# Attention probabilities normalised head by head in a hybrid decoder layer

## The chip, the cores and the metric

The kernel runs on one core of one Trainium2 chip. A core has a tensor engine (PE), a vector engine (DVE), a scalar engine (ACT), a general engine (POOL) and a queue that mostly issues DMAs (SP); each works through its own instructions in program order and waits for the others by semaphores. The metric is the time of the program on the device in microseconds (us). Three runs before the change took 1918.72, 1920.54 and 1920.89 us; the median is 1920.54 us.

## What is computed

One decoder layer on 2048 tokens with 1024 channels: a combined input projection, three mixers side by side (sliding-window attention, short convolution, trailing means), an output projection and a squared-ReLU MLP, with RMS norms around them. The change lies in the attention:

```python
scores = jnp.where(valid[None, :, None, None], scores + bias, NEG)
m = jnp.maximum(jnp.max(scores, axis=-1, keepdims=True), sink)
p = jnp.exp(scores - m)
denom = jnp.sum(p, axis=-1, keepdims=True) + jnp.exp(sink - m)
probs = (p / denom).astype(v.dtype)
out = jnp.einsum('bnhgqk,bnkhd->bnqhgd', probs, v_band)
```

There are 8 query heads and 2 key/value heads. A query block of 128 tokens sees its own 128 keys and the 128 before. The sink adds one column to the denominator.

## The kernel before

Everything is float32. A product of matrices is made of three matmuls on operands that are split into a rounded part and a remainder (`mm3`, L273 to L276: hi by hi, hi by lo, lo by hi). The rounded part of a weight tile is written by ACT (L252, tile `wh`), the remainder (L253, tile `wl`) mostly by POOL, at some places by DVE.

The tokens run in four blocks of 512 (b = 0 to 3). A block has 14 tiles of the input projection (`pj`, eight k-steps of three matmuls each), then 8 tiles of the output projection (`po`). Between the projection tiles lies the attention, in units of one query tile of 128 tokens (j = 0 to 3) and one KV head (g = 0, 1) with its four query heads: a head group. A block has 8 of them, the program 32. The code staggers them: the scores of one unit, the transposes of the unit two tiles back, and its product with the values stand around one projection tile.

A unit runs through the engines like this. PE writes the scores of four heads into PSUM (L582, L583, tile `sc`). For each head DVE adds the bias, scales, and takes the row's extreme (L592, tiles `s` and `nm`); ACT writes the exponential in place and its row sum (L596, tile `den`, which includes the sink's column 256 of `s`, put there by POOL in L585). Then DVE inverts the sums (L599, `rd`) and multiplies the probabilities (L600). PE transposes them per half of the keys (L610, tile `pt`, two PSUM buffers), ACT rounds (L613, `pth`), DVE takes the remainder (L614, `ptl`), PE multiplies by the values (L621, L622, `av`), and ACT and DVE put the result together (L629 to L635, tiles `ao`, `mxh`, `mxl`), which the output projection reads.

DVE does much else between these: in block 0 it scales each projection tile (L523, `z`), in all blocks it works on convolution (L652, `cy`; L659) and means (L694, L700, L701, tile `po`), and on the norm (L318 to L327: small instructions of 128x4). In block 3 it prepares the MLP's operands as well (L769, L815).

The order of the instructions on each engine isn't that of the code: a scheduler places them when the program is built. So a change of a few instructions can reorder others.

Of the kernel before, what the change touches and what calls it, by code (L numbers as in the profile page):

```python
# [15 lines left out]
ALU = mybir.AluOpType  # L16
# [4 lines left out]
P = 128  # L21
# [63 lines left out]
def tile_trunk(  # L85
# [14 lines left out]
    pe, act, dve, gp, sp = nc.tensor, nc.scalar, nc.vector, nc.gpsimd, nc.sync  # L100
# [75 lines left out]
    for j, (r, what) in enumerate(plan):  # L176
# [4 lines left out]
        else:  # L181
            n = what[1]
# [391 lines left out]
    def att_scores(b, j, g):  # L574
        k0 = P if (b == 0 and j == 0) else 0
        n = 2 * P - k0
        sc = ps_sc.tile([P, 4, 2 * P], F32, tag="sc", name=f"sc{b}_{j}_{g}")
        for m in range(4):
            q = Q[b, 2 * g + m // 2]
            w = q[:, m % 2, j * P : (j + 1) * P]  # L580
            c = j * P + k0
            pe.matmul(sc[:, m, k0:], w, Kd[:, 2 * g, c : c + n], start=True, stop=False)  # L582
            pe.matmul(sc[:, m, k0:], w, Kd[:, 2 * g + 1, c : c + n], start=False, stop=True)  # L583
        s = pA.tile([P, 4, 2 * P + 1], F32, tag="s", name=f"s{b}_{j}_{g}", bufs=2)
        gp.tensor_copy(s[:, :, 2 * P], nsink[:, 4 * g : 4 * g + 4])  # L585
        nm = cst.tile([P, 4], F32, tag="nm", name=f"nm{b}_{j}_{g}", bufs=2)
        den = cst.tile([P, 4], F32, tag="den", name=f"den{b}_{j}_{g}", bufs=2)
        rd = cst.tile([P, 4], F32, tag="rd", name=f"rd{b}_{j}_{g}", bufs=2)
        for m in range(4):

            h = 4 * g + m
            dve.tensor_tensor_reduce(  # L592
                out=s[:, m, k0 : 2 * P], in0=sc[:, m, k0:], in1=bias[:, h, k0:], scale=-1.0 / math.sqrt(HD),
                scalar=nsink[:, h : h + 1], op0=ALU.add, op1=ALU.min, accum_out=nm[:, m : m + 1],
            )
            act.activation(  # L596
                s[:, m, k0:], s[:, m, k0:], AF.Exp, bias=nm[:, m : m + 1], scale=-1.0, accum_out=den[:, m : m + 1]
            )
        dve.reciprocal(out=rd, in_=den)  # L599
        dve.tensor_tensor(  # L600
            out=s[:, :, k0 : 2 * P], in0=s[:, :, k0 : 2 * P], in1=rd.unsqueeze(2).to_broadcast([P, 4, n]), op=ALU.mult
        )
        return b, j, g, s

    def att_trans(b, j, g, s):
# [241 lines left out]
    for b in range(NB):  # L847
# [16 lines left out]
        for n, i in enumerate(IN_ORDER[NPRE:]):  # L864
# [15 lines left out]
            if n < 8:  # L880
                st1[n] = att_scores(b, *units[n])
# [356 lines left out]
    for j in range(HC):  # L1238
        if j % 2 == 0:
            sq = pG.tile([P, TH], F32, tag="sq", name=f"sql_{j}", bufs=2)  # L1240
        t = sq[:, j % 2 * w : j % 2 * w + w]
# [86 lines left out]
```

## Time and profile before

| | |
|---|---|
| median of three runs | 1920.54 us |
| profiled execution, its own time | 1918.59 us |
| its span | 1916.8 us |
| clock granted to PE, mean | 0.996 |
| attention of blocks 0, 1, 2, 3 (first to last product of L600) | 58.1 to 112.6, 203.2 to 259.0, 354.4 to 410.3, 528.8 to 577.5 us |

A row of the timeline or of the chain begins with its start and its length in us, both counted in the span. A row of the grouped view ends with the busy time in us, the mean of one instruction in ns and the engine's idle time ahead of the group, with what ended it. A row of a line's view gives the shortest, middle and longest duration in ns. In the table of stretches stand, for each stretch, its length, the busy time and count of PE, PE's weight loads, DVE, ACT and POOL, the clock granted, and the DMA's share and rate. The arrow in a name points from what is read to what is written.

### The profile page before, as it was taken

How to read it: one execution, taken by the hardware profiler on the slowest of the kernel's cores; microseconds unless marked ns; L12 is line 12 of the kernel's file. 1: busy time of each engine (PE TensorE's matmuls, PEld its weight loads, DVE VectorE, ACT ScalarE, POOL GpSimd, SP SyncE). 2: the span in 40 equal slices, each digit the busy share in tenths (PEclk: the TensorE clock that was granted, in tenths of full speed). 3: DMA queues.
4: the chain of work that ended last, by engine and by line, in shares of the span. 5: the costliest groups of instructions: out<-in, count | busy, mean ns of one | idle time of the engine just before them, and what ended most of it. 6: DMA issues, size and time to landing. Idle time of an engine off the chain costs nothing.

```text
span 1916.8 us, 25848 instructions
## 1 busy us (share of the span) xinstructions
PE 1877.0 (98%) x8523; PEld 1521.6 (79%) x8523; DVE 1115.7 (58%) x1615; ACT 896.1 (47%) x1640; POOL 1017.6 (53%) x745
## 2 busy tenths in 40 slices
PE   8999999999899999999999999999999999999998
PEld 5877887887787788888878888888888888888887
DVE  5685675576888577865574444442525264533465
ACT  5664664664376444554565455442323222224332
POOL 5666666565563745554564444434666565526520
PEclk9999999999999999999999999999999999999999
DMA  7327316425936779765685655578777666645344
GB/s 254 102 81 226 102 61 219 121 72 187 308 101 213 238 252 326 265 213 198 223 297 189 198 177 199 185 278 276 236 235 236 195 215 201 220 131 164 100 159 138
DMA packets 194138, 373.36 MB, mean 195 GB/s; under 512 B 22167, under 2 KB 30420, under 8 KB 194004
## 3 DMA queue, kind: packets, MB, share of 16 engines
q1 hardware_dynamic: 193192, 371.10, 59.9%
q8 instruction: 67, 1.10, 0.2%
q10 hardware_dynamic: 812, 0.61, 0.1%
q14 instruction: 67, 0.55, 0.1%
HBM read 248.41 MB, written 116.93 MB: 191 GB/s over the span
## 4 chain that ended last, share of the span: by engine, by line
PE 82%; DVE 8%; DMA 6%; ACT 2%; issue 2%; POOL 0%; SPq 0%; DVEq 0%; ACTq 0%; POOLq 0%
PE o L274 11%; PE o L275 11%; PE o L276 11%; PE bT L275 6%; PE bT L276 6%; PE bT L274 6%; PE bB L275 4%; PE bB L274 4%; PE bB L276 4%; PE pj L275 3%; PE pj L276 3%; PE pj L274 3%; PE po L275 1%; PE po L274 1%; PE po L276 1%
## 5 line engine op out<-in xcount | busy, mean ns | idle before, releaser
L253 POOL TENSOR_TENSOR wl<-wr,wh 128x512 fp32r<-128x512 f32 x354 | 502.5, 1426 | 516.9 <-ACT wh L252 460.0
L252 ACT CAST wh<-wr 128x512 fp32r<-128x512 f32 x416 | 254.1, 617 | 338.1 <-PE bT L275 66.1
L769 DVE TENSOR_TENSOR bl<-br,bh 128x1024 fp32r<-128x1024 f32 (+2 forms) x144 | 185.3, 1290 | 324.4 <-ACT bh L1117 319.6
L275 PE MATMUL o<-bl,wh 128*128 128x512 f32 (+1 forms) x960 | 362.3, 380 | 0.0
L276 PE MATMUL o<-bh,wl 128*128 128x512 f32 (+1 forms) x960 | 361.6, 380 | 0.0
L274 PE MATMUL o<-bh,wh 128*128 128x512 f32 (+1 forms) x960 | 350.2, 380 | 0.0
L275 PEld LDWEIGHTS o<-bl,wh 128*128 128x128 f32 x960 | 180.4, 188 | 37.9 <-DVE bl L769 0.2
L276 PEld LDWEIGHTS o<-bh,wl 128*128 128x128 f32 x960 | 180.3, 188 | 37.8
L274 PEld LDWEIGHTS o<-bh,wh 128*128 128x128 f32 x960 | 175.8, 188 | 38.1 <-ACT bh L1117 0.4
L275 PE MATMUL bT<-hlT,wh 128*128 128x512 f32 x512 | 202.6, 396 | 1.6 <-DVE hlT L973 0.9
L274 PE MATMUL bT<-hhT,wh 128*128 128x512 f32 x512 | 202.2, 395 | 0.2 <-ACT hhT L972 0.2
L276 PE MATMUL bT<-hhT,wl 128*128 128x512 f32 x512 | 202.0, 395 | 0.0
L274 PE MATMUL pj<-xh,wh 128*128 128x512 f32 x440 | 176.7, 403 | 9.5 <-ACT wh L252 6.3
L275 PE MATMUL pj<-xl,wh 128*128 128x512 f32 x440 | 175.6, 399 | 6.7 <-DVE xl L408 6.1
L276 PE MATMUL pj<-xh,wl 128*128 128x512 f32 x440 | 175.4, 399 | 0.5 <-DVE wl L253 0.5
L253 POOL TENSOR_TENSOR wl<-s,wh 128x512 fp32r<-128x512 f32 x64 | 91.3, 1427 | 140.0 <-ACT wh L252 129.5
L252 ACT CAST wh<-s 128x512 fp32r<-128x512 f32 x64 | 39.8, 622 | 248.8 <-PE o L275 248.8
L275 PE MATMUL bB<-hlB,wh 128*128 128x512 f32 x384 | 151.8, 395 | 2.0 <-DVE hlB L973 2.0
L1117 ACT CAST bh<-br 128x1024 fp32r<-128x1024 f32 (+2 forms) x144 | 123.1, 856 | 64.5 <-PE o L276 55.0
L274 PE MATMUL bB<-hhB,wh 128*128 128x512 f32 x384 | 151.6, 395 | 0.0
L276 PE MATMUL bB<-hhB,wl 128*128 128x512 f32 x384 | 151.5, 395 | 0.0
L220 POOL TENSOR_TENSOR s<-wr,wr 128x512 f32<-128x512 f32 x64 | 128.4, 2007 | 14.4 <-DMA wr<-in_w_dram 9.8
(192 smaller groups left out, 3367.5 us busy)
## 6 DMA issues: line engine op xcount, KB each, us to landing
wr<-in_w_dram SPq DMA_DIRECT2D x256, 256.0 KB, 3.6
hop_T<-s SPq DMA_DIRECT2D x128, 256.0 KB, 3.3
wr<-in_win_dram SPq DMA_DIRECT2D x112, 256.0 KB, 4.1
hop_B<-h SPq DMA_DIRECT2D x96, 256.0 KB, 3.3
br<-hop_B SPq DMA_DIRECT2D x48, 512.0 KB, 4.3
br<-hop_T SPq DMA_DIRECT2D x48, 512.0 KB, 3.7
wr<-in_wout_dram SPq DMA_DIRECT2D x64, 256.0 KB, 2.7
wr<-ss_T SPq DMA_DIRECT2D x48, 256.0 KB, 2.9
```

The lines of the kernel that those rows point to most:

```text
L220: gp.tensor_tensor(out=t, in0=a, in1=b, op=op)
L252: act.copy(hi, src)
L253: eng.tensor_tensor(out=lo, in0=src, in1=f32(hi), op=ALU.subtract)
L274: pe.matmul(ps, hi, xh, start=first, stop=False)
L275: pe.matmul(ps, hi, xl, start=False, stop=False)
L276: return pe.matmul(ps, lo, xh, start=False, stop=last)
L769: return dve.tensor_tensor(out=out, in0=a, in1=b, op=ALU.subtract)
L1117: mark["act"] = act.copy(hi, src)
```

## The change

The one reciprocal of the four row sums and the one product over all four heads, in which a sum is repeated along each head's columns, become four pairs: a reciprocal of one column and a product of this head's columns by a scalar per partition. In block 0 the units with j = 0 have only 128 columns per head, all others 256.

```diff
-        dve.reciprocal(out=rd, in_=den)
-        dve.tensor_tensor(
-            out=s[:, :, k0 : 2 * P], in0=s[:, :, k0 : 2 * P], in1=rd.unsqueeze(2).to_broadcast([P, 4, n]), op=ALU.mult
-        )
+        for m in range(4):
+            t = s[:, m, k0 : 2 * P]
+            r = rd[:, m : m + 1]
+            dve.reciprocal(out=r, in_=den[:, m : m + 1])
+            dve.tensor_scalar(out=t, in0=t, scalar1=r, scalar2=None, op0=ALU.mult)
```

Behind these lines each line number is one higher in the changed program (the transposes L610 are L611 there, L614 is L615, L621 and L622 are L622 and L623). The scheduler's order changes with them, most in blocks 0 and 3. On DVE, block 0, unit j = 2, g = 1, stood before (the last two numbers in `rd_2_1` are j and g; the number behind them only counts tiles):

```order
L700 TENSOR_TENSOR po_0_1196<-ps_0_965,prm 64x16
L701 TENSOR_TENSOR po_0_1196<-po_0_1196,pp 64x16
L614 TENSOR_TENSOR ptl_1_1_0_1327<-pt_1_1_0_1321,pth_1_1_0_1326 128x512
L701 TENSOR_TENSOR po_0_1196<-po_0_1196,pp 64x16
L523 TENSOR_TENSOR z_1468<-pj_9_1408,rb_659 128x512
L599 RECIPROCAL rd_2_1_1283<-den_2_1_1282 128x4
L600 TENSOR_TENSOR s_2_1_1279<-s_2_1_1279,rd_2_1_1283 128x4x256
L614 TENSOR_TENSOR ptl_1_1_1_1336<-pt_1_1_1_1330,pth_1_1_1_1335 128x512
L630 TENSOR_TENSOR ao_0_1_1265<-av_0_1_1255,ao_0_1_1265 64x512
```

and at the same place of DVE in the changed program:

```order
L602 RECIPROCAL rd_2_1_1319<-den_2_1_1318 128x1 x2
L603 TENSOR_SCALAR s_2_1_1315<-s_2_1_1315,rd_2_1_1319 128x256 x2
L602 RECIPROCAL rd_2_1_1319<-den_2_1_1318 128x1 x2
L523 TENSOR_TENSOR z_1516<-pj_9_1456,rb_659 128x512
L603 TENSOR_SCALAR s_2_1_1315<-s_2_1_1315,rd_2_1_1319 128x256 x2
L615 TENSOR_TENSOR ptl_1_1_0_1369<-pt_1_1_0_1363,pth_1_1_0_1368 128x512
L631 TENSOR_TENSOR ao_0_1_1301<-av_0_1_1291,ao_0_1_1301 64x512
L615 TENSOR_TENSOR ptl_1_1_1_1378<-pt_1_1_1_1372,pth_1_1_1_1377 128x512
```

The eight instructions stand in pairs, and the remainder `ptl` of the unit before, which stood ahead of the reciprocal, stands behind the products.

On PE, at the end of block 0, the transposes of the second half of unit j = 2, g = 1 stood among the last products of the input projection (`pj_7` is its last tile, `po_0` and `po_1` the first of the output projection):

```order
L610 MATMUL pt_2_1_1_1442<-ident,s_2_1_1279 128x128 x4
L276 MATMUL pj_7_1555<-xh_361,wl_1410 128x512
L274 MATMUL pj_7_1555<-xh_361,wh_1409 128x512
L621 MATMUL av_2_1_1463<-pth_2_1_0_1438,VV 128x512
L622 MATMUL av_2_1_1463<-ptl_2_1_0_1439,VV 128x512
L275 MATMUL pj_7_1555<-xl_362,wh_1409 128x512
L276 MATMUL pj_7_1555<-xh_361,wl_1410 128x512
L274 MATMUL po_0_1608<-mxh,wh_1427 128x512
L274 MATMUL po_1_1659<-mxh,wh_1496 128x512
L610 MATMUL pt_3_1_0_1502<-ident,s_3_1_1376 128x128 x4
```

and in the changed program, on PE at this place:

```order
L276 MATMUL pj_7_1603<-xh_361,wl_1458 128x512
L274 MATMUL po_0_1656<-mxh,wh_1475 128x512
L611 MATMUL pt_2_1_1_1490<-ident,s_2_1_1315 128x128 x4
L622 MATMUL av_2_1_1511<-pth_2_1_0_1486,VV 128x512
L275 MATMUL po_0_1656<-mxl,wh_1475 128x512
L276 MATMUL po_0_1656<-mxh,wl_1476 128x512
L274 MATMUL po_1_1707<-mxh,wh_1544 128x512
L275 MATMUL po_1_1707<-mxl,wh_1544 128x512
L276 MATMUL po_1_1707<-mxh,wl_1545 128x512
L623 MATMUL av_2_1_1511<-ptl_2_1_0_1487,VV 128x512
L611 MATMUL pt_3_1_0_1550<-ident,s_3_1_1418 128x128 x4
```

These transposes now stand behind the last product of `pj_7`, and the first products of the output projection lie between the two products of `av_2_1`.

On PE in block 3, the products of unit j = 1, g = 1 with the values ended, and the transposes of unit j = 2 began, within the last tile of the input projection (`pj_7`; `pj_11` is the tile before it):

```order
L621 MATMUL av_1_1_6003<-pth_1_1_1_5987,VV 128x512
L276 MATMUL pj_11_6132<-xh_4916,wl_5946 128x512
L274 MATMUL pj_11_6132<-xh_4916,wh_5945 128x512
L275 MATMUL pj_11_6132<-xl_4917,wh_5945 128x512
L276 MATMUL pj_11_6132<-xh_4916,wl_5946 128x512
L274 MATMUL pj_7_6213<-xh_4916,wh_5967 128x512
L275 MATMUL pj_7_6213<-xl_4917,wh_5967 128x512
L276 MATMUL pj_7_6213<-xh_4916,wl_5968 128x512
L622 MATMUL av_1_1_6003<-ptl_1_1_1_5988,VV 128x512
L610 MATMUL pt_2_1_0_6086<-ident,s_2_1_5925 128x128 x4
```

and in the changed program, on PE in block 3:

```order
L274 MATMUL pj_11_6324<-xh_5060,wh_6044 128x512
L622 MATMUL av_1_1_6189<-pth_1_1_0_6164,VV 128x512
L623 MATMUL av_1_1_6189<-ptl_1_1_0_6165,VV 128x512
L622 MATMUL av_1_1_6189<-pth_1_1_1_6173,VV 128x512
L623 MATMUL av_1_1_6189<-ptl_1_1_1_6174,VV 128x512
L611 MATMUL pt_2_1_0_6278<-ident,s_2_1_6105 128x128 x4
L275 MATMUL pj_11_6324<-xl_5061,wh_6044 128x512
L276 MATMUL pj_11_6324<-xh_5060,wl_6045 128x512
L274 MATMUL pj_11_6324<-xh_5060,wh_6131 128x512
```

Here both have moved ahead, into the tile before: from behind the first products of `pj_7` to the middle of `pj_11`, whose two weight tiles are `wh_6044` and `wh_6131` in the changed program.

## The prediction

> **What bounds the kernel now.** I read the busy table first, then the table of stretches, then the chain of waits around attention.
>
> ```profile
> PE 1877.0 (98%) x8523; PEld 1521.6 (79%) x8523; DVE 1115.7 (58%) x1615; ACT 896.1 (47%) x1640; POOL 1017.6 (53%) x745
> ...
> core 0: us, PE busy (x) PEld busy (x) DVE busy (x) ACT busy (x) POOL busy (x), PEclk, DMA share, GB/s
> 110.00:120.00 10.00, 10.00 (x48) 7.75 (x46) 9.70 (x15) 4.92 (x11) 6.63 (x6) 1.00 0.18 57
> 120.00:130.00 10.00, 6.31 (x25) 3.86 (x25) 7.70 (x11) 7.83 (x14) 4.55 (x5) 1.00 0.23 74
> 200.00:270.00 70.00, 70.00 (x368) 58.97 (x367) 53.10 (x120) 51.31 (x127) 48.33 (x45) 1.00 0.24 76
> 350.00:420.00 70.00, 70.00 (x367) 58.76 (x366) 52.86 (x119) 50.59 (x126) 47.13 (x44) 1.00 0.24 73
> 575.00:592.00 17.00, 16.52 (x79) 12.81 (x78) 15.89 (x27) 12.16 (x26) 5.21 (x5) 1.00 0.22 71
> ```
>
> PE is the bound: it is busy for 1877.0 of 1916.8 us. The changed lines run only in the attention of the four blocks of 512 tokens, before 600 us, so only PE's idle time there can be won, and only new idle time there can be lost. In blocks 1 and 2 (200 to 270, 350 to 420 us) PE has none. In block 0 PE misses 10.00 − 6.31 = 3.69 us between 120 and 130, in block 3 17.00 − 16.52 = 0.48 us between 575 and 592. The chain shows what ends late in these two places:
>
> ```profile
> 95.91 1.92 DVE s L600
> 105.06 1.65 DVE s L600
> 112.63 1.22 DVE s L600
> 128.88 0.50 PE po L275
> 559.31 1.22 DVE s L600
> 570.39 1.87 DVE s L600
> 577.49 0.33 DVE s L600
> ```
>
> In block 0 the chain runs through DVE from about 90 to 129 us, where the output projection takes over, and three products of L600 stand on it. In block 3 three more do.
>
> **The change: what is removed and added.** Per head group (32 of them: 4 blocks, 4 query tiles, 2 KV heads) one reciprocal of 128x4 and one product of 128x1024 go; four reciprocals of 128x1 and four products of 128x256 come. The arithmetic and the bytes stay.
>
> ```profile
> L599 DVE RECIPROCAL rd<-den 128x4 f32<-128x4 f32 x32 | 5.5, 173 | 15.0 <-ACT s L596 14.9
> L600 DVE TENSOR_TENSOR s<-s,rd 128x1024 f32<-128x1024 f32 x30 | 39.8, 1328 | 0.9
> L600 DVE TENSOR_TENSOR s<-s,rd x32: 893/1225/1923, 58.1 to 577.5; 128x1024 f32<-128x1024 f32 x30, 128x512 f32<-128x512 f32 x2
> L327 DVE SCALAR_TENSOR_TENSOR ny_n<-nt_n,ny_n 128x4 f32<-128x4 f32 x14 | 2.3, 162 | 0.5
> L592 DVE CUSTOM_DVE_ANT_0 s<-sc,bias,nsink x128: 346/480/486, 55.3 to 575.4; 128x256 f32<-128x256 f32 x120, 128x128 f32<-128x128 f32 x8
> 112.43 0.16 DVE L599 RECIPROCAL rd<-den 128x4 f32<-128x4 f32 x1
> 112.63 1.22 DVE L600 TENSOR_TENSOR s<-s,rd 128x1024 f32<-128x1024 f32 x1
> 113.77 0.69 DVE L614 TENSOR_TENSOR ptl<-pt,pth 128x512 fp32r<-128x512 f32 x1
> ```
>
> The last three rows give one group undisturbed, from start to start: 0.20 us from the reciprocal to the product that waits for it, 1.14 us from the product to the next instruction (its 1.22 less an overlap of 0.08). That is 1.34 us.
>
> The new product of 128x256 by a column is in no row. Between 128x4 (0.16, L327) and 128x1024 (1.22) the duration grows by 1.06 us over 1020 elements, so 256 elements come to an estimated 0.42 us, a step of 0.34. The bounds are a step of 0.08 (as short as L327) and of 0.40 (L592, the costliest row of this size). I take 0.34, since it lies on the line of the other products. In the commonest order of the changed program (two reciprocals, two products, then one of each twice), a group costs 0.08 + 0.20 + 0.34 + 0.34 + 0.20 + 0.34 + 0.20 + 0.34 = 2.04 us, **0.70 more** than now. The bounds give 1.00 (0.34 less) and 2.28 (0.94 more); reciprocals of one column whose step is no more than 0.08 either (instead of 0.20, three times) would take off another 0.36.
>
> The second term is what DVE loses to POOL. Three small instructions of the norm (L320, L325, L326) show it:
>
> ```profile
> L320 DVE TENSOR_SCALAR ny_n<-nt_n x7: 151/792/889, 28.8 to 503.7; 128x4 int32<-128x4 int32 x7
> L325 DVE TENSOR_TENSOR nt_n<-ny_n 128x4 f32<-128x4 f32 x21 | 9.0, 430 | 0.7
> L326 DVE TENSOR_TENSOR nt_n<-nt_n,nv_n 128x4 f32<-128x4 f32 x21 | 8.7, 416 | 0.7
> 293.06 1.21 DVE L326 TENSOR_TENSOR nt_n<-nt_n,nv_n 128x4 f32<-128x4 f32 x1
> ...
> 292.97 1.29 POOL L253 TENSOR_TENSOR wl<-wr,wh 128x512 fp32r<-128x512 f32 x1
> ```
>
> An instruction on four elements takes 1.21 us when a POOL instruction has started just before it (292.97, 1.29 us), and ends with that one: DVE stands still for a whole POOL instruction, however small its own work. L320 is the same operation as the new product, and it is held too (0.151 to 0.889). So four short products are four chances to be held where there was one. The price per chance: L325 and L326 lose 0.27 and 0.25 us on average against 0.162, L327 right behind them nothing, 0.17 in the mean. Four products lose 0.70, L600 lost 0.10 (mean 1328 less median 1225), so **0.60 more** per group. Bounds: 0.10 less (never held), and 4.1 more (each held for 1.05, as above).
>
> [...]
>
> Sum on DVE: +0.70 + 0.60 = **+1.3 us per group**, between −0.8 and +5.0.
>
> **What of it lies beside other work.** In block 1 the finished group waits long for its transposes:
>
> ```profile
> 239.73 0.39 PE L275 MATMUL pj<-xl,wh 128*128 128x512 f32 x1
> 239.96 0.39 PE L276 MATMUL pj<-xh,wl 128*128 128x512 f32 x1
> 240.88 1.03 PE L610 MATMUL pt<-ident,s 128*128 128x128 f32 x8
> 241.41 1.43 DVE L600 TENSOR_TENSOR s<-s,rd 128x1024 f32<-128x1024 f32 x1
> 249.14 1.04 PE L610 MATMUL pt<-ident,s 128*128 128x128 f32 x8
> ```
>
> The product ends at 242.84, its transposes start at 249.14: 6.3 us of slack against 1.3. DVE is busy for 53.10 of 70 us with 70/8.26 = 8.5 groups (PE's transposes come at 240.88 and again 8.26 us later), and 8.5 x 1.3 = 11 more still fit. Blocks 1 and 2 cost nothing as long as a group adds less than (70 − 53.1)/8.5 = 2.0 us; beyond that PE waits for DVE there.
>
> The finer grain itself brings little: the order shows the transposes of a group mostly in one piece behind the last head. What the four reciprocals wait for is each head's exponential (L596). Queued behind such a wait on DVE are the products and then the splits L614, which PE's L622 waits for. Before, one reciprocal waited for all four, 14.9 us in all (the L599 row); where it waited, the first heads' products now fall into that time.
>
> Block 0, 90 to 129 us: three groups on the chain, 3 x 1.3 = 3.9 us. Behind the last product DVE has gaps that take some of it up:
>
> ```profile
> 121.21 0.69 DVE L614 TENSOR_TENSOR ptl<-pt,pth 128x512 fp32r<-128x512 f32 x1 [1.22 <-ACT pth L613]
> 122.74 0.69 DVE L614 TENSOR_TENSOR ptl<-pt,pth 128x512 fp32r<-128x512 f32 x1 [0.24 <-ACT pth L613]
> 124.09 1.00 DVE L652 SCALAR_TENSOR_TENSOR cy<-uu,prm,cy 128x512 f32<-128x512 f32 x1 [0.66 <-ACT cy L650]
> ```
>
> 1.22 + 0.24 + 0.66 = 2.1 us, which leaves **+1.8 us**. The order fits: there the second half of a group's transposes moves behind the last projection, so PE has less to fill the wait with.
>
> Block 3: again three groups, 3.9 us, against this slack:
>
> ```profile
> 575.84 0.68 DVE L614 TENSOR_TENSOR ptl<-pt,pth 128x512 fp32r<-128x512 f32 x1
> 579.82 0.39 PE L622 MATMUL av<-ptl,VV 128*128 128x512 f32 x1
> ```
>
> The split ends at 576.52 and is read at 579.82: 3.3 us. That leaves **+0.6 us**. PE's rows there now stand some 17 projection products earlier, about 3.9 us at 0.23 us each (239.73 to 239.96), so this slack may be gone; up to 3 us more is kept for the range. PE, ACT, POOL and the DMA queues issue the same instructions as before, partly in another order.
>
> Sum: +1.8 + 0.6 = +2.4 us. The profiled execution took 1918.59 us, 1.95 under the median of 1920.54; it goes to 1921.0, the median to **1922.9 us**.
>
> **Rivals.** How L600 fared in block 1 stands ahead, since two of them turn on it:
>
> ```profile
> L600 DVE TENSOR_TENSOR s<-s,rd x8: 1211/1226/1433, 203.2 to 259.0; 128x1024 f32<-128x1024 f32 x8
> ```
>
> *DVE saturates (slower).* If the four products meet a busy POOL each time, a group passes the 2.0 us from which blocks 1 and 2 become DVE-bound. POOL is busy for 48.33 of 70 us there, which speaks for it; that L600 was hardly held in block 1 (at most 1433 against 1226 ns) speaks against. At +2.5 per group: 16 groups x 0.5 = 8, block 0 7.5 − 2.1 = 5.4, block 3 7.5 − 3.3 = 4.2, together +18: 1938 us.
>
> *Short products (faster).* At the lower bounds a group saves up to 0.8 us, the three of block 0 2.4 of the 3.69 us that PE misses, block 3 at most its 0.48; −2.9, and with all of both regained −4.2: 1916.3 to 1917.6 us. For it: the DVE waits that the early heads fill. Against: POOL's hold in the rows above.
>
> *Hidden.* Long products that are never held cost a group 0.70 − 0.10 = 0.6 more, short ones that are held as L325 to L327 were −0.34 + 0.60 = 0.3; three times that is less than the 2.1 us of block 0 and the 3.3 of block 3, and nothing shows: 1920.5 ± 1.5 us. For it speaks that the row of a tensor_scalar (L320) has only four elements, so that length and hold were never seen together; against it, that three products in a row stand on the chain of block 0.
>
> That the change does not do what it says is excluded by the order: it lists the reciprocals of one column and the products apart.
>
> **How the numbers follow.** About 0.2%, 3.84 us, is what a measurement of this kernel can tell from no change. My forecast, a loss of 0.5 to 6 us: 0.42 (0.32 within 0.2%, 0.10 beyond). Saturated: 0.20, slower. Hidden: 0.22, same. Short: 0.16 (0.12 faster, 0.04 same). So faster 0.12, same 0.58, slower 0.30. The range leaves out half of the saturated and half of the short case: 1917.5 to 1931; the forecast alone 1921 to 1926.5.
>
> **What would show it.** The mean of the new product (0.42 plus 0.17), some of them held at over 1 us; DVE's busy time 32 x 1.3 = 42 us up; PE still full at 200 to 270; its gap at 120 to 130 grown from 3.7 to 5.5. I am wrong if PE shows gaps in blocks 1 and 2, if products run at 0.3 us or less, or if PE's gap shrinks.

## The result, and the profile after

The changed kernel took 1930.88 us in the median of 8 runs (1924.76 to 1938.45), the kernel before 1918.14 us beside it (8 runs, 1911.84 to 1921.65). The ratio is 1.0069, 95% interval 1.0055 to 1.0083: 13 us slower. The profiled execution took 1938.45 us, the longest of the eight, and was granted a clock of 0.989; that of the kernel before took 1918.59 us at 0.996. So the two traces lie further apart than usual runs do.

The busy table and the stretches of the changed kernel (columns as before):

```profile
PE 1888.8 (98%) x8523; PEld 1529.4 (79%) x8523; DVE 1158.4 (60%) x1807; ACT 896.5 (46%) x1640; POOL 1003.1 (52%) x745
...
110.00:120.00 10.00, 9.50 (x44) 7.80 (x45) 9.69 (x26) 6.28 (x16) 5.55 (x5) 1.00 0.17 52
120.00:130.00 10.00, 5.34 (x25) 3.90 (x24) 7.19 (x12) 5.67 (x10) 5.75 (x6) 0.85 0.32 90
200.00:270.00 70.00, 70.00 (x370) 59.03 (x369) 59.93 (x170) 47.52 (x121) 41.73 (x42) 1.00 0.26 82
350.00:420.00 70.00, 70.00 (x368) 58.87 (x368) 61.82 (x171) 47.59 (x122) 41.80 (x42) 1.00 0.31 89
540.00:550.00 10.00, 6.13 (x32) 4.83 (x31) 10.00 (x21) 4.68 (x13) 6.22 (x6) 1.00 0.51 161
575.00:592.00 17.00, 16.00 (x87) 13.31 (x85) 16.75 (x38) 11.03 (x28) 9.30 (x10) 1.00 0.16 49
```

The span grew by 1936.7 − 1916.8 = 19.9 us. It has two parts. PE's busy time went up by 1888.8 − 1877.0 = 11.8 us with the same 8523 matmuls: they ran at a lower clock (0.989 in the mean against 0.996). The other 8.1 us are added idle time. In blocks 1 and 2 (200 to 270, 350 to 420) PE is still full, though DVE has taken on 7 to 9 us there. The gap at 120 to 130 grew from 3.69 to 4.66 us, and one stands at 540 to 550 (3.87 us) where PE had none at the same work of block 3.

The new instructions, grouped by form:

```profile
L603 DVE TENSOR_SCALAR s<-s,rd 128x256 f32<-128x256 f32 x120 | 82.3, 712 | 1.3
L602 DVE RECIPROCAL rd<-den 128x1 f32<-128x1 f32 x128 | 16.6, 152 | 0.7 <-ACT s L596 0.3
L603 DVE TENSOR_SCALAR s<-s,rd 128x128 f32<-128x128 f32 x8 | 4.1, 528 | 0.1
```

and the view of the product's line, with its shortest, middle and longest duration:

```profile
L603 DVE TENSOR_SCALAR s<-s,rd x128: 269/356/3573, 57.2 to 594.3; 128x256 f32<-128x256 f32 x120, 128x128 f32<-128x128 f32 x8
```

The normalisation takes 82.3 + 16.6 + 4.1 = 103.0 us by these groups, but a reciprocal begins some 0.08 us before the product ahead of it ends, so this sum counts some time twice. The stretch of the attention, with the instructions alone that read or write `rd` (length, DVE's busy time and count, clock, DMA), shows them without it, before and after:

```profile
0.00:620.00 620.00, 48.01 (x64) 0.99 0.51 157
0.00:620.00 620.00, 97.12 (x256) 0.98 0.48 149
```

That is 1.50 us per group before and 3.03 us after, 1.53 us more. The middle product takes 0.356 us, the mean one of 128x256 0.712 and the longest 3.57. The timeline of DVE and of POOL in block 1 shows what the difference is:

```profile
233.84 0.15 DVE L602 RECIPROCAL rd<-den 128x1 f32<-128x1 f32 x1
234.02 1.01 DVE L603 TENSOR_SCALAR s<-s,rd 128x256 f32<-128x256 f32 x1
234.95 0.15 DVE L602 RECIPROCAL rd<-den 128x1 f32<-128x1 f32 x1
235.14 1.40 DVE L603 TENSOR_SCALAR s<-s,rd 128x256 f32<-128x256 f32 x1
...
233.84 1.04 POOL L673 TENSOR_TENSOR ps<-ps 64x512 f32<-64x512 f32 x1
235.09 1.29 POOL L376 TENSOR_TENSOR acc<-acc,sq 128x512 f32<-128x512 f32 x1
```

The first product ends at 235.03, POOL's instruction at 234.88; the second at 236.54, POOL's at 236.38. Each of the two ends 0.15 us behind the POOL instruction that began before it. Of the 128 products 52 took over 0.45 us, all 52 beside a POOL instruction, and 49 of them end 0.15 to 0.16 us behind one. None of the 128 reciprocals was held (at most 0.17 us); nor was a single L592, which reads its scores from PSUM (at most 0.49 us).

### The profile page after: what moved, and what is told of

Read it like the earlier page. It is cut to its first block, busy times and chain, and to the rows that moved or that the text cites. A ratio compares the mean times of both kernels' runs of the same rounds, so it can differ in the third digit from the quotient of the medians.

```text
span 1936.7 us, 26062 instructions
## 1 busy us (share of the span) xinstructions
PE 1888.8 (98%) x8523; PEld 1529.4 (79%) x8523; DVE 1158.4 (60%) x1807; ACT 896.5 (46%) x1640; POOL 1003.1 (52%) x745
## 4 chain that ended last, share of the span: by engine, by line
PE 79%; DVE 10%; DMA 7%; issue 1%; ACT 1%; POOL 1%; SPq 1%; DVEq 0%; ACTq 0%; POOLq 0%
PE o L274 11%; PE o L275 11%; PE o L276 11%; PE bT L275 6%; PE bT L276 6%; PE bT L274 6%; PE bB L275 4%; PE bB L276 4%; PE bB L274 4%; PE pj L275 3%; PE pj L274 3%; PE pj L276 3%; DVE s L603 2%; PE po L274 1%; PE po L275 1%
## 5 line engine op out<-in xcount | busy, mean ns | idle before, releaser
L253 POOL TENSOR_TENSOR wl<-wr,wh 128x512 fp32r<-128x512 f32 x354 | 493.4, 1399 | 537.4 <-ACT wh L252 481.7
```

Source lines behind the costliest of these rows:

```text
L253: eng.tensor_tensor(out=lo, in0=src, in1=f32(hi), op=ALU.subtract)
```

## The experiments

The theories at the start were these: the loss lies in the instructions (the products are held by POOL, and DVE is late), or in the new order that the scheduler makes around them. To part them, some kernels take their order from a table: every engine's instructions are queued as in the kernel before ("old order") or as in the changed kernel ("new order"), by edges that set only the order of issue:

```diff
+    for d in seq[k + 1 : k + 1 + count]:
+        at += d
+        for i in items[at]:
+            if last is not None:
+                tc.add_manual_dep(
+                    i,
+                    last.name,
+                    mybir.DependencyInfo(mybir.DependencyClass.NoSync, mybir.DependencyReason.DATA),
+                    reason="order",
+                )
+            last = i
```

Times are medians; the ratio is to the kernel before, run beside it (1916.3 to 1919.6 us). Differences in us below are the ratios, taken of 1918 us.

| kernel | us | ratio, 95% interval | DVE per group, us |
|---|---|---|---|
| before | 1918.1 | 1 | 1.50 |
| changed | 1930.9 | 1.0069 (1.0055 to 1.0083) | 3.03 |
| new_ops_old_order | 1934.1 | 1.0080 (1.0063 to 1.0096) | 3.22 |
| old_ops_new_order | 1931.8 | 1.0061 (1.0045 to 1.0078) | 1.75 |
| tt_new_order | 1936.0 | 1.0087 (1.0070 to 1.0104) | 3.36 |
| one_recip_old_order | 1925.5 | 1.0032 (1.0018 to 1.0047) | 2.32 |
| recips_ahead_old_order | 1924.4 | 1.0037 (1.0023 to 1.0050) | 2.42 |
| one_recip_four_ts | 1933.7 | 1.0089 (1.0071 to 1.0107) | 2.62 |
| four_recip_one_tt | 1923.2 | 1.0022 (1.0011 to 1.0033) | 1.97 |
| long_product_old_order | 1955.3 | 1.0203 (1.0184 to 1.0221) | 3.44 |
| inner_blocks | 1919.2 | 1.0011 (1.0000 to 1.0022) | |
| outer_blocks | 1929.6 | 1.0066 (1.0054 to 1.0079) | |
| outer_old_order | 1930.9 | 1.0078 (1.0063 to 1.0093) | |
| block_0 | 1918.7 | 1.0009 (0.9999 to 1.0020) | |
| block_3 | 1924.4 | 1.0037 (1.0024 to 1.0051) | |
| act_half | 1921.3 | 1.0015 (1.0002 to 1.0027) | |
| act_products | 1915.0 | 0.9985 (0.9972 to 0.9997) | |
| the same again | 1916.8 | 0.9991 (0.9977 to 1.0004) | |
| act_two_tt_two | 1917.9 | 0.9995 (0.9981 to 1.0008) | |
| act_outer | 1918.1 | 1.0001 (0.9992 to 1.0011) | |

The last column is DVE's busy time in the instructions that read or write `rd`, as in the two rows above, over 32 groups; for long_product_old_order the added product is counted too. Each value comes from one profiled execution.

### Instructions or order

The four pairs, issued in the place of the old reciprocal and product, in the old order:

> The changed instructions, queued on every engine as the kernel before queues them; only the reciprocal and the product of a group are replaced, in their place, by the four pairs. If the loss comes from the products themselves (held by POOL, mean near 0.7 us), most of it stays: 8 to 14 us slower than before, the products' mean 0.65 to 0.75 us. If it comes from the new order, this runs within 3 us of before. If both have a share, 3 to 8 us slower.

The two instructions of before in the new order, the product where the last of the four stands:

> The instructions of before, queued on every engine as the changed kernel queues them; the one product stands where the last of the four stands. If the products themselves make the loss: within 3 us of before. If the new order makes it: 8 to 14 us slower than before. If both have a share: 3 to 8 us slower.

Each alone costs about as much as the whole change: 15 and 12 us. They don't add up, so neither theory holds as the only cause. In the old order the new instructions make PE wait even in blocks 1 and 2, as its view of waits from 200 to 430 us shows (total, times, longest):

```profile
PE av L625 <- DVE ptl L617: 4.9, 4, 1.5
```

In the new order PE's transposes of a group's first heads stand early, and the one product behind the last head is late for them. Its gaps at 99.6 us (2.2 us) and 533.6 us (2.5 us) wait for L600, so part of its loss is due to where that product was put; this run doesn't tell what the order costs by itself.

One reciprocal and four products were run in both orders, without that flaw (the lines are against the changed kernel):

```diff
+        dve.reciprocal(out=rd, in_=den)
         for m in range(4):
             t = s[:, m, k0 : 2 * P]
-            r = rd[:, m : m + 1]
-            dve.reciprocal(out=r, in_=den[:, m : m + 1])
-            dve.tensor_scalar(out=t, in0=t, scalar1=r, scalar2=None, op0=ALU.mult)
+            dve.tensor_scalar(out=t, in0=t, scalar1=rd[:, m : m + 1], scalar2=None, op0=ALU.mult)
```

> One reciprocal of 128x4 as before, four products by a scalar per partition, all queued as in the kernel before. Three reciprocals fewer take 0.2 to 0.5 us off a group. If the products make the loss: within 3 us of the kernel with all new instructions in the old order. If the reciprocals have a share: over 3 us faster than that one.

> One reciprocal and four products by a scalar per partition, in the order that the scheduler makes for them. The same instructions in the order of the kernel before took 1925.5 us. If the loss lies in the instructions: 1922 to 1929 us here too. If a new order adds its own loss: 1930 us or more; if the scheduler's order makes up for part: below 1922.

6 us slower than before in the old order, 17 in the scheduler's own. So an order can cost 11 us, though not all of it by itself: in the scheduler's order 43 of these products took over 0.45 us, in the old order 36. For the four pairs it does not: 15 us in the old order, 13 in their own, with intervals that overlap.

### What holds the products

The changed kernel's order, with `dve.tensor_tensor(out=t, in0=t, in1=r.to_broadcast([P, n]), op=ALU.mult)` for each product:

> The changed kernel's order on every engine, with a tensor_tensor (the column repeated) in place of each tensor_scalar. If only the tensor_scalar is shut out by POOL: products of 0.40 to 0.50 us in the mean and none over 1 us, and 4 to 10 us faster than the changed kernel (1921 to 1927). If a tensor_tensor is held alike: 0.70 to 0.85 us in the mean, and 0 to 5 us slower than the changed kernel (1931 to 1936). If the order alone counts: within 3 us of the changed kernel.

Then the four reciprocals ahead of the four products, in the old order (against the changed kernel):

```diff
-        for m in range(4):
-            t = s[:, m, k0 : 2 * P]
-            r = rd[:, m : m + 1]
-            dve.reciprocal(out=r, in_=den[:, m : m + 1])
-            dve.tensor_scalar(out=t, in0=t, scalar1=r, scalar2=None, op0=ALU.mult)
+        for m in range(4):
+            dve.reciprocal(out=rd[:, m : m + 1], in_=den[:, m : m + 1])
+        for m in range(4):
+            t = s[:, m, k0 : 2 * P]
+            dve.tensor_scalar(out=t, in0=t, scalar1=rd[:, m : m + 1], scalar2=None, op0=ALU.mult)
```

> All new instructions in the order of the kernel before, as in the first run, but the four reciprocals of a group stand ahead of its four products instead of between them. If a reciprocal between two products lets a POOL instruction in, which then holds the next product: about 36 of the 128 products over 0.45 us (53 when they alternate), their mean near 0.60 us, and a time within 3 us of the kernel with one reciprocal (1922 to 1929). If the reciprocals cost by their own duration: about 53 held and 1931 to 1937 us.

Products in the grouped view: first tensor_tensor in the new order, then, in the old order, the pairs, the reciprocals ahead, and one reciprocal:

```profile
L604 DVE TENSOR_TENSOR s<-s,rd 128x256 f32<-128x256 f32 x120 | 92.6, 798 | 1.2
```

```profile
L604 DVE TENSOR_SCALAR s<-s,rd 128x256 f32<-128x256 f32 x120 | 87.0, 725 | 4.3
```

```profile
L602 DVE TENSOR_SCALAR s<-s,rd 128x256 f32<-128x256 f32 x120 | 63.3, 589 | 0.0
```

```profile
L602 DVE TENSOR_SCALAR s<-s,rd 128x256 f32<-128x256 f32 x120 | 65.7, 610 | 1.1
```

A tensor_tensor is held alike: 57 of 128, 0.41 us when it isn't (the middle one of the 128 takes 0.43 us, the longest 3.71). With the reciprocals out from between the products 35 of 128 are held, with one reciprocal 36, with alternating pairs 53. In these runs the number of reciprocals hardly matters (1924.4 us with four ahead, 1925.5 with one), their place does: moved ahead, they give back 8 of 15 us. In the changed kernel 31 of the 67 products right behind a reciprocal are held, 11 of the 41 behind another product, and 10 of the 20 behind other work of DVE. The author's reading: POOL starts its next instruction while DVE runs a reciprocal, and the next product meets it. The trace shows this for 12 of the 31; for 13 the POOL instruction had begun before the reciprocal, and for 6 it began after the product. No run takes work away from POOL, so that it is POOL which holds the products rests on where they end, and on this pair of runs.

The reverse, four reciprocals with the one product of before (scheduler's order):

> Four reciprocals of one column and the one product of before, in the scheduler's own order. If the loss comes from four products that can be held: 1917 to 1924 us. If the reciprocals by themselves have a share: 1925 us or more.

1923.2 us lies in the range of the first answer. A loss of 4 us stays all the same (0.22%, interval 0.11 to 0.33%); the product's mean is 1479 ns here against 1328.

To see whether DVE's time counts whatever it is made of, the kernel before in its own order got a second long instruction per group:

```diff
+        t = s[:, :, k0 : 2 * P]
+        dve.tensor_tensor(out=t, in0=t, in1=t, op=ALU.max)
```

> The instructions and the order of the kernel before, with one more instruction behind each product: the larger of the probabilities and themselves, 128x1024, which changes no value and takes DVE another 1.15 to 1.3 us a group (2.65 to 2.9 us in all, against 1.49). If DVE's time per group is what counts, whatever it is made of: 8 to 13 us slower than before, on the line of the runs in the same order (2.3 to 2.4 us: about 6; 3.2 us: 15). If only short products that POOL holds make the loss: within 4 us of before.

Neither: 39 us slower. Its grouped lines, and one group on DVE and on POOL:

```profile
L602 DVE TENSOR_TENSOR s<-s 128x1024 f32<-128x1024 f32 x30 | 55.4, 1848 | 1.0
L601 DVE TENSOR_TENSOR s<-s,rd 128x1024 f32<-128x1024 f32 x30 | 45.3, 1509 | 1.0
```

```profile
244.91 3.32 DVE L601 TENSOR_TENSOR s<-s,rd 128x1024 f32<-128x1024 f32 x1
248.26 2.31 DVE L602 TENSOR_TENSOR s<-s 128x1024 f32<-128x1024 f32 x1
...
244.84 1.05 POOL L673 TENSOR_TENSOR ps<-pp 128x526 f32<-128x526 f32 x1
245.86 1.28 POOL L253 TENSOR_TENSOR wl<-wr,wh 128x512 fp32r<-128x512 f32 x1
247.10 1.18 POOL L585 COPY s<-nsink 128x4 f32<-128x4 f32 x1
248.24 1.25 POOL L636 TENSOR_TENSOR mxl<-ao,mxh 64x512 fp32r<-64x512 f32 x1
```

Long products are held too: the second starts behind a POOL instruction that began 0.02 us earlier, and ends 1.08 us behind it. POOL is held in turn: its copy of four columns (L585) starts at 247.10 and ends at 248.28, 0.05 us behind the first product, 1.18 us in all; the one at 241.65 in the same profile takes 0.20 us, and the middle one of the 32 in the kernel before 0.19 us. With 3.44 us a group DVE is little busier than with the four pairs in this order (3.22), and the loss is 39 us instead of 15. At least two things differ, and the runs don't part them: the four pairs can start before the last head's exponential (DVE waited 0.2 us in all ahead of the pairs' reciprocals, 13.1 us ahead of this kernel's), and these long products hold POOL up. So DVE's busy time by itself doesn't set the loss.

### Where the loss arises

The change in some of the blocks and the old lines in the others, in the scheduler's own order, and once in the old order (the condition is `b in (1, 2)`, `b in (0, NB - 1)` twice, `b == 0` and `b == NB - 1`):

```diff
+        if b in (1, 2):
+            for m in range(4):
...
+        else:
+            dve.reciprocal(out=rd, in_=den)
...
```

> The change in blocks 1 and 2 alone, in the scheduler's own order. If PE's slack there hides it, as predicted: within 2.5 us of before. If the inner blocks have a share: 4 us slower or more.

> The change in blocks 0 and 3 alone, in the scheduler's own order. If the whole loss arises there: 9 to 14 us slower than before. If the inner blocks have a share of a third or more: below 8 us.

> The change in blocks 0 and 3 alone, every engine queued as in the kernel before. The profile with all four blocks changed in that order is 12 us behind at the end of block 3, of which 4 to 5 arise in the inner blocks: so 7 to 11 us slower than before if the instructions make the loss; within 3 us if the outer blocks lose only by their new order.

> The change in block 0 alone, in the scheduler's own order. By the profile of the run with both outer blocks changed (7 us behind at the end of block 0, 2 to 3 of them regained later): 4 to 7 us slower than before. By the prediction's term: 1.8 us.

> The change in block 3 alone, in the scheduler's own order. By the same profile (another 8 to 10 us lost between 515 and 690 us): 6 to 10 us slower than before. By the prediction's term: 0.6 us.

Blocks 1 and 2 cost 2.1 us, with no change at the end of the interval, block 0 1.7 us, with no change inside it, block 3 7.1 us. Blocks 0 and 3 together cost 12.7 us, 4 more than the two apart; the intervals allow it. The clock points the same way: the runs' mean is 0.9922 with both, against 0.9945 for the kernel before beside them (0.0023 of 1918 us, an estimated 4 us), and 0.9936 and 0.9937 with one of them, against 0.9939. In the old order the two blocks cost no less (15 us), so the new order isn't needed for the loss. PE's waits in block 3 when only that block is changed, from 515 to 600 us:

```profile
PE av L629 <- DVE ptl L621: 2.3, 1, 2.3
PE pt L617 <- DVE s L604: 1.9, 1, 1.9
PE ppm L274 <- DVE ptl L621: 0.9, 1, 0.9
PE po L274 <- ACT mxh L720: 0.7, 1, 0.7
```

### Taking the products from DVE

Two of the four products on ACT; all four; all four timed again; two on ACT and two in one tensor_tensor; all four in blocks 0 and 3 alone:

```diff
+        dve.reciprocal(out=rd, in_=den)
         for m in range(4):
             t = s[:, m, k0 : 2 * P]
+            act.activation(t, t, AF.Copy, scale=rd[:, m : m + 1])
```

With two on ACT beside the changed kernel's pairs, and beside one tensor_tensor:

```diff
+            if m % 2:
+                act.activation(t, t, AF.Copy, scale=r)
+            else:
+                dve.tensor_scalar(out=t, in0=t, scalar1=r, scalar2=None, op0=ALU.mult)
```

```diff
+        dve.tensor_tensor(
+            out=s[:, 2:, k0 : 2 * P], in0=s[:, 2:, k0 : 2 * P], in1=rd[:, 2:].unsqueeze(2).to_broadcast([P, 2, n]), op=ALU.mult
+        )
+        for m in range(2):
+            t = s[:, m, k0 : 2 * P]
+            act.activation(t, t, AF.Copy, scale=rd[:, m : m + 1])
```

> The changed kernel, with the products of two of the four heads on ACT, in the scheduler's own order. If DVE's load counts: half of the loss goes, 1920 to 1927 us. If the order alone counts: 1928 to 1934 us, as the changed kernel.

> One reciprocal; the four products on ACT (a copy with a scale per partition), in the scheduler's own order. If DVE's time in blocks 0 and 3 sets their end: DVE loses 1.3 us a group against the kernel before and the time falls to 1912 to 1918 us. If ACT becomes the late one, or the new order costs more than DVE gains: 1923 us or more.

> The four products on ACT, timed again beside its neighbours. If its first time holds: 1912 to 1918 us and an interval below 1.000. If that was chance: within 2 us of the kernel before.

> One reciprocal, the products of two heads on ACT and those of the other two in one tensor_tensor of 128x512 on DVE, in the scheduler's own order. If less on DVE is what helps and ACT (62 of 70 us in block 1 when it has all four) is the next limit: as fast as all four on ACT or up to 3 us faster, 1911 to 1917 us. If only a DVE without these products helps, since a product behind a POOL instruction is held: 1916 to 1921 us.

> The products of blocks 0 and 3 on ACT, those of blocks 1 and 2 as before, in the scheduler's own order. If DVE's time in the outer blocks is what counts: 1912 to 1917 us, as fast as with ACT everywhere or faster. If the inner blocks gain too: 1917 to 1920 us.

Two products fewer on DVE give back most of the loss (1921.3 us). With all on ACT, from 90 to 130 and from 195 to 280 us:

```profile
90.00:130.00 40.00, 37.23 (x183) 29.58 (x182) 35.33 (x70) 33.95 (x77) 25.50 (x25) 1.00 0.21 65
195.00:280.00 85.00, 83.97 (x431) 69.70 (x430) 48.21 (x119) 69.31 (x169) 50.58 (x51) 1.00 0.28 84
```

PE misses 2.77 us in the end of block 0, against 40.00 − 36.31 = 3.69 before, and 1.03 us in block 1, where it missed none. The first timing lay below the kernel before by 0.15%, the second by 0.09% with 1.0 inside its interval; the last two kernels can't be told from before. So there is at most 0.1 to 0.2% in it, and no version here is clearly better than before; all are better than the change.

## Why the prediction was wrong in size

*The price per group: near, in part by luck.* 1.53 us measured, +1.3 forecast, within its wide bounds. The parts were off against each other: the product that isn't held takes 0.35 us, not 0.42, and the hold costs 0.712 − 0.356 = 0.36 in the mean, not 0.17. Four holds less the 0.10 of before are 1.3 us a group, not 0.60, which leaves 0.2 us for the longer work, not 0.70. DVE's busy time rose by 1158.4 − 1115.7 = 42.7 us (42 said), and that is luck too: the changed lines added 97.1 − 48.0 = 49.1 us, and the rest of DVE's work took 6.4 us less beside them. What the prediction didn't see is that the reciprocals, which it priced by their duration, go with products that are held more often.

Products of both kinds were held, 52 of 128 as tensor_scalar and 57 of 128 as tensor_tensor. The lower bound of their length, a step of 0.08 us, wasn't reached: the shortest product of 128x256 took 0.33 us, a step of 0.25 with the overlap of 0.08 taken off, the middle one 0.36 (the 0.269 in the row above is one of 128x128).

*Blocks 1 and 2 hidden: nearly right.* PE stays full from 200 to 270 and from 350 to 420 us; alone they cost 2.1 us, at the edge of what was measured.

*Block 0, +1.8 us: the time right, in part by luck.* It costs 1.7 us alone (interval −0.2 to 3.8). In that run's own profile PE idles 30.00 − 24.56 = 5.44 us from 100 to 130, 1.75 more than before (3.69), as forecast. But half clock follows, from 124.92 to 135.16, where PE is busy for 8.91 us; half of that, about 4 us, is lost as well, and no term stood for it. The measured time grew by less because PE then does without idle time that it had before: 1.75 us from 200 to 330, where it now has none, and more behind. In the changed kernel the gap at 120 to 130 went to 4.66 us, not 5.5, and the stretch from 100 to 130 to 6.47.

*Block 3, "The split ends at 576.52 and is read at 579.82: 3.3 us. That leaves +0.6 us": this step failed.* It costs 7.1 us alone. The slack was read at the last group of the block. Most of the loss arises at the first groups, ahead of the three that the chain named: in the run with block 3 alone PE's two long waits (1.86 and 2.30 us) end at 526.98 and 539.07 us. There the slack is smaller. There stood before, on DVE and on PE:

```profile
534.94 1.86 DVE L600 TENSOR_TENSOR s<-s,rd 128x1024 f32<-128x1024 f32 x1
536.72 1.28 DVE L614 TENSOR_TENSOR ptl<-pt,pth 128x512 fp32r<-128x512 f32 x2
537.95 0.39 PE L622 MATMUL av<-ptl,VV 128*128 128x512 f32 x1
```

and after:

```profile
543.72 2.24 DVE L603 TENSOR_SCALAR s<-s,rd 128x256 f32<-128x256 f32 x2
545.88 0.21 DVE L602 RECIPROCAL rd<-den 128x1 f32<-128x1 f32 x2
546.07 2.48 DVE L603 TENSOR_SCALAR s<-s,rd 128x256 f32<-128x256 f32 x2
548.47 1.27 DVE L615 TENSOR_TENSOR ptl<-pt,pth 128x512 fp32r<-128x512 f32 x2
549.20 0.50 PE L623 MATMUL av<-ptl,VV 128*128 128x512 f32 x1 [3.87 <-DVE ptl L615]
```

Before, the first of the two splits ends at about 537.36 (half of 1.28 us behind 536.72) and is read at 537.95: 0.6 us of slack, not 3.3. After, the products, with two reciprocals between, take 548.47 − 543.72 = 4.75 us instead of 536.72 − 534.94 = 1.78, and PE stands for 3.87 us. That is 3.0 us more on this one group, where the forecast had 1.3 for each: the price is a mean, and POOL is at work through nearly all of these four products (4.46 of the 4.75 us). DVE is full there (9.87 of 10 us from 525 to 535 before) with the MLP's operands L769 between the groups, so nothing takes the time up. A part is the order: seven products of the projection stood between this `ptl` product and its `pth` product before, now three, which at 0.23 us each leaves PE 0.9 us less to do.

*Blocks together.* The forecast had 0 + 1.8 + 0.6 = 2.4 us. Alone, the parts cost 2.1 + 1.7 + 7.1 = 10.9 of the 13 us; the rest is not placed by these runs; that the clock takes it is likely by the means above, not shown. That 1930.88 us still lies inside the stated range (1917.5 to 1931) is luck: its upper part stood for blocks 1 and 2 becoming DVE-bound, which did not happen.

*The clock: no term of the sum.* Here idle time of PE is followed by a slower clock (0.50 in two of the stretches below). The stretches at the end of block 0, after, cut where the clock changes:

```profile
120.10:123.52 3.42, 2.35 (x14) 1.76 (x12) 3.33 (x7) 1.07 (x2) 1.28 (x1) 1.00 0.22 77
123.52:126.93 3.41, 1.40 (x6) 1.00 (x7) 1.45 (x3) 2.14 (x5) 2.56 (x3) 1.00 0.25 77
126.93:130.35 3.42, 1.84 (x7) 1.34 (x6) 2.64 (x4) 2.35 (x4) 2.08 (x4) 0.50 0.54 140
130.35:133.76 3.41, 3.41 (x9) 2.38 (x9) 2.96 (x5) 1.30 (x2) 0.02 (x1) 0.50 0.04 13
133.76:137.17 3.41, 3.41 (x17) 2.73 (x16) 2.46 (x5) 2.95 (x6) 0.68 (x1) 1.00 0.28 77
```

and the worst such stretch at that place before:

```profile
122.97:126.38 3.41, 1.98 (x8) 1.13 (x7) 2.69 (x4) 2.42 (x4) 2.17 (x3) 1.00 0.40 125
```

PE idles for 3.41 − 1.40 = 2.01 us of one stretch, and the next two run at half clock: 9 matmuls fit where 17 fit later. Before, the worst stretch there has 1.43 us idle and nothing follows. The profiled execution has six such spells ahead of its last microseconds, the kernel before one. Over the runs the mean clock is 0.9923 (8 runs) against 0.9943 (12 runs of before, beside the first experiments): 0.002 of 1930 us, an estimated 4 of the 13 us. It goes with how the idle time is gathered: new_ops_old_order, whose four waits for `ptl` in blocks 1 and 2 are of at most 1.5 us each, kept 0.9947 and lost its 15 us without a slower clock.

*The rivals.* "DVE saturates" fell: blocks 1 and 2 stayed full. "Hidden" and "short products" fell because the hold is worth 1.3 us a group.

## What to carry to other kernels

Here one long DVE instruction became four short ones beside a POOL that is busy for 60 to 69% of blocks 1 and 2, and each of the four took 0.36 us more in the mean than the middle one, about a quarter of a POOL instruction (the middle one there takes 1.29 us). Where a trace shows POOL as busy, start from such a price for each short instruction. With the reciprocals, of which none was held, out from between the products 35 of 128 were held instead of 53 (1924.4 us instead of 1934.1): look for such instructions between short ones, and move them ahead. Read the slack of a stage at each of its units, not at the last, and take the smallest. Where the tensor engine is the bound, add to new idle time the clock that it costs (here an estimated 4 of the 13 us), above all when it falls in one lump.

## What the runs showed of the hardware

The clock fell on a grid of 3.41 us. The six spells at half clock in the profile of the changed kernel ahead of its last microseconds begin at 126.93, 184.96, 488.74, 519.46, 550.18 and 676.48 us, that is 17, 89, 9, 9 and 37 times 3.413 us apart, and last 6.83 or 3.41 us. With the grid laid from the first slow spell of each of the 20 profiles, take the windows at full clock from 50 us up to the spell that ends each profile. All 49 in which PE idled for more than 1.9 us were followed by half clock for 3.4 us or a multiple; of the 160 with 0.95 to 1.9 us idle 20 were, and of those below 0.95 us none. In the profiles of before and after alone it was all 5, 2 of 14, and none of 1061. (The spell at the very end is another matter: in 15 of the 20 profiles PE idled less than 0.95 us in the window before it, 0.31 us in the changed kernel's, and the runs don't show why.) So what counted here is how much idle time fell into one window: more than 1.9 us was enough each time.

By where their instructions end, DVE and POOL held each other up, in both directions. A held product of 128x256 (tensor_scalar, changed kernel) ended 0.15 us behind POOL's instruction, and a tensor_tensor of that size was held as well (57 of 128 in tt_new_order). In long_product_old_order the tensor_tensor of 128x1024 at 248.26 us ended 1.08 us behind POOL's, and a copy of four columns on POOL (1.18 us instead of 0.20) 0.05 us behind the product of 128x1024. A reciprocal of one column was never held (at most 0.17 us, 128 of them), nor an L592 (at most 0.49 us).
